# Where four prefetched weight tiles lie in an fp32 decoder trunk: two raw tiles more in spare result tiles, and a transposition moved by two k-tiles

## The chip, the cores and the metric

The kernel runs on one core of a Trainium2 chip. The metric is device time in microseconds (us) of one launch, lower is better. TensorE (PE, weight loads PEld) multiplies into PSUM banks; VectorE (DVE) and ScalarE (ACT) work elementwise; GpSimd (POOL) has a few tiny instructions; SyncE (SP) issues every load of weights, in one queue, in order. Each engine runs its own instructions in order and waits on semaphores for the others.

## The reference

Two decoder layers over 256 tokens of width 2048, all float32. Layer 0 mixes tokens by retention (8 heads, keys of 256, values of 512), layer 1 by latent attention (16 heads). After each mixer comes a SwiGLU block of width 5632, and each of the four parts is wrapped in two root-mean-square norms:

```python
h = rms_norm(x, norm_ffn_pre[i])
gate, up = jnp.split(h @ w_gu, [D_FF], axis=-1)
x = x + rms_norm((jax.nn.silu(gate) * up) @ w_down, norm_ffn_post[i])
```

The change touches retention's input products (`x @ w_in`, split into q, k, v and g) and this gate-and-up product.

## The kernel before

**Float32 by three products.** Tokens stand in two tiles of 128. Every weight tile (128 rows of k by 1024 columns, 512 KB) is loaded raw, and split into a high part (ACT, a cast) and a low part (DVE, raw minus high). A product is high x high, high x low and low x high: three matmuls of 512 columns for each token tile and each half of the columns, twelve for a k-tile.

**Groups.** The gate-and-up weights are cut into 11 groups, named `gu` 0 to 10, of 1024 columns (512 of gate, 512 of up) and 16 k-tiles. Retention has 4 query/key groups (`rqk`) and 8 value/gate groups (`rvg`). Group 0 of a kind that follows a norm runs by `group`; the others by `first_sevens`: there the first pairs of k-tiles (4 pairs in gate and up, 2 and 3 in retention) are multiplied by Strassen's scheme, with seven products instead of eight. For a pair the weights come as `s0` (a raw tile) and `s1` (a tile of tag `y4`); DVE forms the sums `ta` (L448, L452) and `t` (L449, later L463), and the parts `b`, `a`, `c`, `d`, each with hi and lo, are splits of these. In the names of the profile these are `gu_bhi`, `gu_blo` and so on. When the pairs are through, four DVE instructions combine the banks (L475, L478, L482, L485, with ACT copies L471 and L479 into `mv`). Then k-tiles 8 to 15 of gate and up follow one by one as `w8` to `w15`.

**Rings of tiles.** There are 4 raw tiles, 5 pairs of hi and lo, 6 banks of tag `mm`, of which a group takes 4, and 4 tiles of tag `y4`. A raw tile is free again when its last split or sum has been made, a hi/lo pair when its last matmul has read it.

**Spare tiles.** The result of a group's activation, transposed, is kept until the down product: 11 tiles `aT` of 128 x 1024 in gate and up (8 tiles `yT` in retention). While fewer groups are done, tiles of this ring are empty. The kernel lends them to the last k-tiles of a group for their hi and lo parts (names `xhi`, `xlo`): with j groups done, `min(2, (groups - j) // 2)` k-tiles get such a pair, so two in gate and up from group 0 to 7, one in 8 and 9, none in 10. Retention's query/key groups have two tiles of their own for this (one k-tile).

**End of a group.** For each token tile ACT makes silu of the gate bank (`fsg`), DVE multiplies with the up bank (L995, into `fa`), then TensorE transposes four blocks into a bank of tag `misc` (L962, `ftp`), and ACT copies them to `aT` (L963). The transposes are put off with `later(2 + t, ...)`: a count of k-tiles begun, so they are written down in the third and fourth k-tile of the next group. The final order of each engine is made by a scheduler from the order of writing, its priorities and free tiles; the order on each queue is shown below where it matters.

**Names in the tables:** `gu_w_raw` loads at L544, `gu_s` at L440 and L443; casts at L204, low parts at L205, all matmuls at L409.

Of the kernel before, what the change touches and what calls it, by code (L numbers as in the profile page):

```python
# [8 lines left out]
F32 = mybir.dt.float32  # L9
F32R = mybir.dt.float32r  # L10
# [5 lines left out]
P = 128  # L16
SEQ = 256
D = 2048
DT = D // P
NT = SEQ // P  # L20
EPS = 1e-6
RH, RK, RV = 8, 256, 512
# [35 lines left out]
def trunk(  # L58
# [73 lines left out]
    def later(k, fn):  # L132
        order[0] += 1
        todo.append((steps[0] + k, order[0], fn))
# [63 lines left out]
    wp = ctx.enter_context(tc.tile_pool(name="wp", bufs=1))  # L198
    RAW, WB, MV = 4, 5, 6

    def split(hi, lo, src, g=None):

        if g is None:
            nc.scalar.copy(out=hi, in_=src)  # L204
            nc.vector.tensor_sub(out=lo, in0=src, in1=hi.bitcast(F32))  # L205
        else:
            nc.scalar.activation(out=hi, in_=src, func=AF.Copy, scale=g)
            nc.vector.scalar_tensor_tensor(
                out=lo, in0=src, scalar=g, in1=hi.bitcast(F32), op0=ALU.mult, op1=ALU.subtract
            )  # L210

    def weights(load, parts, name, room=None):

        raw = wp.tile([P, 1024], F32, tag="raw", bufs=RAW, name=f"{name}_raw")
        load(raw)
        if room is None:
            hi = wp.tile([P, 1024], F32R, tag="whi", bufs=WB, name=f"{name}_hi")
            lo = wp.tile([P, 1024], F32R, tag="wlo", bufs=WB, name=f"{name}_lo")
        else:
            hi, lo = room(f"{name}_xhi"), room(f"{name}_xlo")  # L220
# [309 lines left out]
        carry_out(plan, banks, cols, {})  # L530
        return banks

    def tile_load(w, g, name, halves=0, spare=(0, None)):

        def load(kt, first_half=False):
            n = 512 if kt < halves or first_half else 1024

            def dma(raw):
                for a in range(0, 1024, 512 if kt < halves else 1024):
                    m = 512 if kt < halves else 1024
                    nc.sync.dma_start(out=raw[:, a : a + m], in_=w[g, kt, :, a : a + m])  # L544

            parts = [(a, n, None) for a in range(0, 512 if first_half else 1024, n)]
            return weights(dma, parts, f"{name}_w{kt}", spare[1] if kt >= DT - spare[0] else None)

        return load

# [186 lines left out]
    def retention():  # L737
# [40 lines left out]
        def vg_group(h, spare):  # L778
            return first_sevens(h_lhs, DT, ret_vg, h, f"rvg{h}", VG_SEVENS, lambda p: ins[p], spare)

        with tc.tile_pool(name="rt_s", bufs=1) as sp:
# [63 lines left out]
            with tc.tile_pool(name="rt_q", bufs=1) as rp:  # L845
                rope_c = rp.tile([P, NT, NF_R], F32, name="rope_c")
                rope_s = rp.tile([P, NT, NF_R], F32, name="rope_s")
                spare = 1, lambda name: rp.tile([P, 1024], F32R, tag="spare", bufs=2, name=name)
                for gq in range(4):
                    banks = qk_group(gq, spare)  # L850
                    if gq == 0:
                        rx = [rms(first[t], D, "rx", f"first_r{t}") for t in range(NT)]
                        rotary_tables()
                        for t in range(NT):
                            for dst, src in ((rope_c, cos_t), (rope_s, sin_t)):
                                nc.vector.tensor_scalar(
                                    dst[:, t, :], src[:, t, 0:NF_R], scalar1=rx[t], scalar2=None,
                                    op0=ALU.mult,
                                )
                    head_scores(gq, rotated(banks, rope_c, rope_s, rp), rp)  # L860
                banks = vg_group(0, spare)

            with tc.tile_pool(name="rt_v", bufs=1) as rp:

                yT = {}

                def spare_y(name):
                    return rp.tile([P, 1024], F32R, tag="yT", bufs=RH, name=name)

                def take_y(k0, n):  # L870
                    return yT[k0 // 4][:, k0 % 4 : k0 % 4 + n]
# [73 lines left out]
    def swiglu(i):  # L945
        with tc.tile_pool(name=f"ff{i}", bufs=1) as fp:

            groups = FF // 512
            aT = {}

            def spare_a(name):
                return fp.tile([P, 1024], F32R, tag="aT", bufs=groups, name=name)

            def take_a(k0, n):
                return aT[k0 // 4][:, k0 % 4 : k0 % 4 + n]
# [23 lines left out]

            for j in range(groups):  # L980
                name = f"gu{i}_{j}"
                spare = min(2, (groups - j) // 2), spare_a
                if j:
                    banks = first_sevens(
                        h_lhs, DT, w_gu[i], j, name, GU_SEVENS, lambda p: ins[p], spare
                    )
                else:
                    banks = group(h_lhs, DT, tile_load(w_gu[i], j, name, 0, spare), name, lead=4)
                watch[0] = None
                both = fp.tile([P, NT, 512], F32, tag="fa", bufs=1, name="fa")  # L990
                for t in range(NT):
                    sg = fp.tile([P, 512], F32, tag="fsg", bufs=2, name="fsg")
                    nc.scalar.activation(out=sg, in_=banks[t][0], func=AF.Silu, scale=rx_next[t])
                    a = both[:, t, :]
                    nc.vector.scalar_tensor_tensor(  # L995
                        out=a, in0=banks[t][1], scalar=rx_next[t], in1=sg, op0=ALU.mult, op1=ALU.mult
                    )
# [282 lines left out]


    retention()
    swiglu(0)
    mla()
    swiglu(1)


# [89 lines left out]
```

## Time and profile before

| what | value |
|---|---|
| median of 3 runs | 2427.02 us (2423.98 to 2428.43) |
| profiled execution's own time | 2426.71 us |
| span of its instructions | 2424.9 us |
| granted TensorE clock, mean over the span | 0.998 |
| busy: TensorE, DVE, ACT | 99%, 88%, 61% of the span |
| read from HBM | 459.64 MB, 190 GB/s over the span |
| gate-and-up groups 1 to 10, layer 0 and layer 1 | 426.69 us and 424.95 us |
| the seven retention value groups 1 to 7 | 313.57 us |

A line of a group or a wait names engine, line of the kernel, what is written and read, and times in us; `<-` after a bracket or a name is what ended the wait. A row of the windows view has the stretch, its length, then for PE, PEld, DVE, ACT and POOL busy us and, in brackets, the number of instructions; then the granted clock, the share of time that the 16 DMA engines were busy, and GB/s. A row of the timeline has the start, the duration, engine, line, operation, tiles and the count of equal instructions merged; in square brackets the engine's idle time before it and what ended it. Matmuls overlap: a duration of 0.39 us is that of one in the pipeline, and the pace is read from start to start.

### The profile page before, as it was taken

The numbers are of one execution on the slowest core, as the hardware profiler recorded it, in microseconds if no ns is written. First come the engines' busy times: TensorE is split into PE (matmuls) and PEld (weight loads), VectorE is DVE, ScalarE is ACT, GpSimd is POOL, SyncE is SP. The second block draws the span as 40 slices with busy tenths as digits, with TensorE's granted clock in tenths as the row PEclk, the third lists the DMA queues.
The fourth block names the chain that finished last, engine by engine and source line by source line (L and its number), as shares of the span: only waits on it lengthen the run. The fifth ranks groups of instructions, "written<-read, shape, count | busy, mean of one in ns | idle before, by whom it ended". The sixth has DMA issues, their size and how long they took to land.

```text
span 2424.9 us, 30707 instructions
## 1 busy us (share of the span) xinstructions
PE 2403.3 (99%) x10888; PEld 1975.1 (81%) x10888; DVE 2122.0 (88%) x3034; ACT 1479.1 (61%) x2082; POOL 23.9 (1%) x38
## 2 busy tenths in 40 slices
PE   9999999999999999999999999999999999999998
PEld 7888888888888787888888888888877888888887
DVE  8878989887879999899989987876899999998997
ACT  6545666665656666666666665655666666666664
POOL 0000000000000000000000000000000000000000
PEclk9999999999999999999999999999999999999999
DMA  7565565556665565656456654446656565556655
GB/s 273 171 211 185 164 206 194 165 172 203 192 213 193 195 213 184 217 172 216 168 194 214 207 185 148 130 137 198 202 182 215 180 211 202 188 183 202 206 194 164
DMA packets 129610, 463.75 MB, mean 191 GB/s; under 512 B 14640, under 2 KB 15024, under 8 KB 129456
## 3 DMA queue, kind: packets, MB, share of 16 engines
q1 hardware_dynamic: 129456, 461.80, 57.7%
q8 instruction: 85, 1.39, 0.2%
q14 instruction: 69, 0.57, 0.1%
HBM read 459.64 MB, written 2.10 MB: 190 GB/s over the span
## 4 chain that ended last, share of the span: by engine, by line
PE 80%; DVE 12%; DMA 4%; issue 2%; ACT 2%; SPq 0%; POOL 0%; DVEq 0%; ACTq 0%; POOLq 0%
PE gu_b L409 23%; PE dn_b L409 16%; PE rvg_b L409 14%; PE rto_b L409 6%; PE rqk_b L409 5%; PE mlo_b L409 3%; PE q L409 3%; PE dn_m L409 3%; DMA gu_w_raw<-w_gu 2%; DVE gu_blo L205 2%; DVE gu_alo L205 1%; PE mc_b L409 1%; DVE gu_w_lo L205 1%; DVE gu_t L449 1%; DVE gu_clo L205 1%
## 5 line engine op out<-in xcount | busy, mean ns | idle before, releaser
L409 PE MATMUL gu_b<-gu_w_hi,hT 128*128 128x512 f32 x1248 | 342.0, 390 | 0.0
L409 PEld LDWEIGHTS gu_b<-gu_w_hi,hT 128*128 128x128 f32 x1248 | 233.1, 188 | 49.0 <-DVE hT L205 0.9
L204 ACT CAST dn_w_hi<-dn_w_raw 128x1024 fp32r<-128x1024 f32 (+1 forms) x176 | 172.8, 993 | 95.2 <-DMA dn_w_raw<-w_down 44.4
L205 DVE TENSOR_TENSOR gu_w_lo<-gu_w_raw,gu_w_hi 128x1024 fp32r<-128x1024 f32 x156 | 185.5, 1218 | 48.4 <-ACT gu_w_hi L204 48.3
L204 ACT CAST gu_w_hi<-gu_w_raw 128x1024 fp32r<-128x1024 f32 x156 | 158.1, 1048 | 92.9 <-DMA gu_w_raw<-w_gu 73.2
L205 DVE TENSOR_TENSOR dn_w_lo<-dn_w_raw,dn_w_hi 128x1024 fp32r<-128x1024 f32 (+1 forms) x176 | 196.1, 1146 | 9.2 <-ACT dn_w_hi L204 8.9
L409 PE MATMUL gu_b<-gu_w_lo,hT 128*128 128x512 f32 x624 | 193.3, 390 | 0.0
L409 PE MATMUL dn_b<-dn_w_hi,dn_ah 128*128 128x512 f32 x536 | 169.3, 390 | 0.0
L409 PE MATMUL dn_b<-dn_w_lo,dn_ah 128*128 128x512 f32 x536 | 169.0, 389 | 0.0
L409 PE MATMUL dn_b<-dn_w_hi,dn_al 128*128 128x512 f32 x536 | 168.9, 389 | 0.0
L409 PE MATMUL rvg_b<-rvg_w_hi,hT 128*128 128x512 f32 x552 | 149.8, 390 | 0.0
L409 PEld LDWEIGHTS gu_b<-gu_w_lo,hT 128*128 128x128 f32 x624 | 116.6, 188 | 25.3 <-DVE gu_w_lo L205 1.3
L409 PEld LDWEIGHTS rvg_b<-rvg_w_hi,hT 128*128 128x128 f32 x552 | 103.4, 188 | 21.4
L409 PEld LDWEIGHTS dn_b<-dn_w_hi,dn_al 128*128 128x128 f32 x536 | 100.6, 188 | 21.0
L409 PEld LDWEIGHTS dn_b<-dn_w_lo,dn_ah 128*128 128x128 f32 x536 | 100.6, 188 | 20.9
L409 PEld LDWEIGHTS dn_b<-dn_w_hi,dn_ah 128*128 128x128 f32 x536 | 100.3, 188 | 20.4
L409 PE MATMUL rqk_b<-rqk_w_hi,hT 128*128 128x512 f32 x384 | 106.0, 392 | 2.2 <-ACT rqk_w_hi L204 1.5
L204 ACT CAST gu_ahi<-gu_ta 128x1024 fp32r<-128x1024 f32 x80 | 84.3, 1054 | 35.1 <-DVE gu_ta L452 17.1
L205 DVE TENSOR_TENSOR rvg_w_lo<-rvg_w_raw,rvg_w_hi 128x1024 fp32r<-128x1024 f32 x69 | 82.3, 1222 | 25.5 <-ACT rvg_w_hi L204 25.1
L204 ACT CAST gu_bhi<-gu_t 128x512 fp32r<-128x512 f32 x80 | 49.7, 621 | 85.9 <-DVE gu_t L449 85.8
L204 ACT CAST rvg_w_hi<-rvg_w_raw 128x1024 fp32r<-128x1024 f32 x69 | 71.1, 1051 | 46.0 <-DMA rvg_w_raw<-ret_vg 34.7
L205 DVE TENSOR_TENSOR gu_alo<-gu_ta,gu_ahi 128x1024 fp32r<-128x1024 f32 x80 | 97.7, 1221 | 0.0
(487 smaller groups left out, 6109.5 us busy)
## 6 DMA issues: line engine op xcount, KB each, us to landing
gu_w_raw<-w_gu SPq DMA_DIRECT2D x192, 512.0 KB, 4.3
dn_w_raw<-w_down SPq DMA_DIRECT2D x176, 512.0 KB, 4.4
gu_s<-w_gu SPq DMA_DIRECT2D x160, 512.0 KB, 4.4
rvg_w_raw<-ret_vg SPq DMA_DIRECT2D x80, 512.0 KB, 4.4
rto_w_raw<-ret_out SPq DMA_DIRECT2D x64, 512.0 KB, 4.4
rqk_w_raw<-ret_qk SPq DMA_DIRECT2D x51, 512.0 KB, 4.5
rvg_s<-ret_vg SPq DMA_DIRECT2D x48, 512.0 KB, 4.3
mlo_w_raw<-mla_out SPq DMA_DIRECT2D x32, 512.0 KB, 3.6
```

Of the source, the lines that this page charges most:

```text
L204: nc.scalar.copy(out=hi, in_=src)
L205: nc.vector.tensor_sub(out=lo, in0=src, in1=hi.bitcast(F32))
L409: nc.tensor.matmul(out, e[2](), e[3](), start=bank not in begun, stop=ends[bank, added.get(bank, 0)] == n, skip_group_check=bank in added,)
L449: nc.vector.tensor_add(out=t2[p], in0=ta[:, 0:512], in1=b11)
```

## The change

A function `share(slots, room)` replaces the two-tile rule. With `slots` empty result tiles it gives `both` k-tiles a hi/lo pair (two from 6 slots on, one from 3 on, else none), and up to two of the remaining tiles hold **raw** weights (names `xraw`): of k-tiles 12 and 13, or of 13 alone. Gate and up thus have 2 pairs and 2 raws in groups 0 to 5, 1 pair and 2 raws in 6 and 7, 1 and 1 in 8, 0 and 2 in 9, 0 and 1 in 10. Retention's value groups 1 and 2 have 2 and 2, 3 and 4 have 1 and 2, 5 has 1 and 1, 6 has 0 and 2, 7 has 0 and 1. The query/key groups and value group 0 get a third tile: 1 pair and 1 raw. And the transposes of the gate-and-up activations are put off by `later(4 + t, ...)`.

```diff
+    def share(slots, room):
+        both = 2 if slots >= 6 else 1 if slots >= 3 else 0
+        return min(2, slots - 2 * both), both, room
...
-    def weights(load, parts, name, room=None):
-        raw = wp.tile([P, 1024], F32, tag="raw", bufs=RAW, name=f"{name}_raw")
+    def weights(load, parts, name, raw_room=None, room=None):
+        if raw_room is None:
+            raw = wp.tile([P, 1024], F32, tag="raw", bufs=RAW, name=f"{name}_raw")
+        else:
+            raw = raw_room(F32, f"{name}_xraw")
...
-            return weights(dma, parts, f"{name}_w{kt}", spare[1] if kt >= DT - spare[0] else None)
+            raws, both, room = spare
+            return weights(
+                dma, parts, f"{name}_w{kt}", room if DT - 2 - raws <= kt < DT - 2 else None,
+                room if kt >= DT - both else None,
+            )
...
-                spare = 1, lambda name: rp.tile([P, 1024], F32R, tag="spare", bufs=2, name=name)
+                spare = share(3, lambda kind, name: rp.tile([P, 1024], kind, tag="spare", bufs=3, name=name))
...
-                        banks = vg_group(h, (min(2, (RH - h) // 2), spare_y))
+                        banks = vg_group(h, share(RH - h, spare_y))
...
-                spare = min(2, (groups - j) // 2), spare_a
+                spare = share(groups - j, spare_a)
...
-                    later(2 + t, lambda j=j, t=t, a=a: transposes(j, t, a))
+                    later(4 + t, lambda j=j, t=t, a=a: transposes(j, t, a))
```

No instruction is added or removed, and none changes its size. The scheduler makes a new order from it. Lines move too: L440, L443 and L544 become L449, L452 and L554; L205, L449, L452, L463 and L995 become L210, L458, L461, L472 and L1009; L409 and L962 become L418 and L976.

**SyncE's queue from group 5 to group 6 of layer 0.** `gu_5_w_raw` are k-tiles 8 to 11 and then 12 to 15; of the `gu_6_s` loads the first four are `s1`, the last four `s0` of the next group. Before:

```order
L544 DMA gu_5_w_raw<-w_gu 128x1024 x4
L443 DMA gu_6_s_8833<-w_gu 128x1024
L443 DMA gu_6_s_8874<-w_gu 128x1024
L443 DMA gu_6_s_8905<-w_gu 128x1024
L443 DMA gu_6_s_8936<-w_gu 128x1024
L544 DMA gu_5_w_raw<-w_gu 128x1024 x4
L440 DMA gu_6_s_8831<-w_gu 128x1024
```

Of the change:

```order
L554 DMA gu_5_w_raw<-w_gu 128x1024 x4
L554 DMA gu_5_w_xraw<-w_gu 128x1024 x2
L452 DMA gu_6_s_8833<-w_gu 128x1024
L452 DMA gu_6_s_8861<-w_gu 128x1024
L452 DMA gu_6_s_8905<-w_gu 128x1024
L452 DMA gu_6_s_8936<-w_gu 128x1024
L554 DMA gu_5_w_raw<-w_gu 128x1024 x2
L449 DMA gu_6_s_8831<-w_gu 128x1024
```

The loads of k-tiles 12 and 13 moved ahead of the four `s1` loads; 14 and 15 stayed behind them.

**DVE where the activation of group 5 is made, among the sums and low parts of group 6.** `fa` is the activation, `s_8934` and `s_8936` belong to the fourth pair. Before:

```order
L205 TENSOR_TENSOR gu_6_blo<-gu_6_s_8903,gu_6_bhi 128x512
L452 TENSOR_TENSOR gu_6_ta<-gu_6_s_8903,gu_6_s_8905 128x512
L205 TENSOR_TENSOR gu_6_blo<-gu_6_t_8908,gu_6_bhi 128x512
L448 TENSOR_TENSOR gu_6_ta<-gu_6_s_8934 128x512
L995 SCALAR_TENSOR_TENSOR fa<-gu_5_b_8460,rto_x_r,fsg 128x512
L449 TENSOR_TENSOR gu_6_t_8939<-gu_6_ta,gu_6_s_8936 128x512
L995 SCALAR_TENSOR_TENSOR fa<-gu_5_b_8462,rto_x_r,fsg 128x512
L452 TENSOR_TENSOR gu_6_ta<-gu_6_s_8934,gu_6_s_8936 128x512
L463 TENSOR_TENSOR gu_6_t_8836<-gu_6_t_8836,gu_6_s_8833 128x512
L205 TENSOR_TENSOR gu_6_alo<-gu_6_ta,gu_6_ahi 128x1024
```

Of the change:

```order
L210 TENSOR_TENSOR gu_6_blo<-gu_6_t_8908,gu_6_bhi 128x512
L457 TENSOR_TENSOR gu_6_ta<-gu_6_s_8934 128x512
L461 TENSOR_TENSOR gu_6_ta<-gu_6_s_8934,gu_6_s_8936 128x512
L458 TENSOR_TENSOR gu_6_t_8939<-gu_6_ta,gu_6_s_8936 128x512
L472 TENSOR_TENSOR gu_6_t_8836<-gu_6_t_8836,gu_6_s_8833 128x512
L472 TENSOR_TENSOR gu_6_t_8864<-gu_6_t_8864,gu_6_s_8861 128x512
L1009 SCALAR_TENSOR_TENSOR fa<-gu_5_b_8460,rto_x_r,fsg 128x512
L472 TENSOR_TENSOR gu_6_t_8908<-gu_6_t_8908,gu_6_s_8905 128x512
L1009 SCALAR_TENSOR_TENSOR fa<-gu_5_b_8462,rto_x_r,fsg 128x512
L210 TENSOR_TENSOR gu_6_alo<-gu_6_ta,gu_6_ahi 128x1024
```

The two activations moved behind the sums of the fourth pair and behind three of the four L463 (now L472).

**TensorE in the first pairs of group 6.** `ftp` are the transposes of group 5's activation. Before:

```order
L409 MATMUL gu_6_b_8829<-gu_6_alo,sh_6615 128x512
L409 MATMUL gu_6_b_8829<-gu_6_ahi,sl_6616 128x512
L962 MATMUL ftp_8860<-cst,fa 128x128 x4
L962 MATMUL ftp_8868<-cst,fa 128x128 x4
L409 MATMUL gu_6_b_8827<-gu_6_bhi,hT 128x512
```

Of the change:

```order
L418 MATMUL gu_6_b_8830<-gu_6_alo,sh_6615 128x512
L418 MATMUL gu_6_b_8830<-gu_6_ahi,sl_6616 128x512
L976 MATMUL ftp_8891<-cst,fa 128x128 x4
L976 MATMUL ftp_8899<-cst,fa 128x128 x4
L418 MATMUL gu_6_b_8827<-gu_6_bhi,hT 128x512
```

The transposes moved from behind the first pair's nine matmuls to behind the second pair's twelve; the bank `b_8830`, which the second pair is the first to write, now comes ahead of them. Later in groups 1 to 4 of both layers the `chi,sh` matmuls now stand ahead of the first `dhi,hT` one, as they did in groups 5 to 10; in group 10 it is the other way round.

More of the change, by code (lines that the diff above doesn't have):

```diff
@@ L219, in weights @@
         else:
-            hi, lo = room(f"{name}_xhi"), room(f"{name}_xlo")
+            hi, lo = room(F32R, f"{name}_xhi"), room(F32R, f"{name}_xlo")
         for a, n, g in parts:
@@ L531, in first_sevens, with tile_load @@
         return banks
-    def tile_load(w, g, name, halves=0, spare=(0, None)):
+    def tile_load(w, g, name, halves=0, spare=(0, 0, None)):
         def load(kt, first_half=False):
@@ L865, in retention, with spare_y @@
                 yT = {}
-                def spare_y(name):
-                    return rp.tile([P, 1024], F32R, tag="yT", bufs=RH, name=name)
+                def spare_y(kind, name):
+                    return rp.tile([P, 1024], kind, tag="yT", bufs=RH, name=name)
                 def take_y(k0, n):
@@ L949, in swiglu, with spare_a @@
             aT = {}
-            def spare_a(name):
-                return fp.tile([P, 1024], F32R, tag="aT", bufs=groups, name=name)
+            def spare_a(kind, name):
+                return fp.tile([P, 1024], kind, tag="aT", bufs=groups, name=name)
             def take_a(k0, n):
```

## The prediction

> **What bounds the kernel now.** I read the page first, then the list of waits of TensorE's loads, then the windows of single groups, then the timeline of one group's end. The page says that TensorE is busy 99% of the span. So I ask first which stages have TensorE time to give back at all.
>
> ```profile
> PE 2403.3 (99%) x10888; PEld 1975.1 (81%) x10888; DVE 2122.0 (88%) x3034; ACT 1479.1 (61%) x2082; POOL 23.9 (1%) x38
> PEld gu_b L409 <- ACT gu_mv L479: 5.8, 8, 0.9
> PEld ftp L962 <- DVE fa L995: 5.3, 13, 0.8
> PEld gu_b L409 <- DVE gu_b L482: 5.3, 12, 0.7
> PEld gu_b L409 <- DVE gu_clo L205: 2.7, 7, 0.5
> PEld gu_b L409 <- DVE gu_dlo L205: 1.7, 3, 0.7
> ACT gu_w_hi L204 <- DMA gu_w_raw<-w_gu: 73.2, 45, 3.4
> ```
>
> The five PEld lines (total us, times, longest) are the longest waits of TensorE inside the gate-and-up groups: all for VectorE (DVE), or for a ScalarE (ACT) copy behind it. The last line is of ACT, and comes back below. They hold the 0.04 to 0.23 us that lie before any load, so their sum is too high. The loss itself I take from lengths of groups. The first three rows below are groups 1, 6 and 7 of the first layer, from one first matmul to the next; the two "sum" rows add groups 1 to 10 of the first and of the second layer; the fourth is the seven value-and-gate groups of retention.
>
> ```profile
> 780.84:823.83 42.99, 42.40 (x190) 34.38 (x188) 40.76 (x54) 27.54 (x37) 0.00 (x0) 1.00 0.56 197
> 995.19:1037.04 41.85, 41.85 (x189) 34.51 (x188) 38.08 (x49) 26.34 (x34) 0.00 (x0) 1.00 0.62 201
> 1037.04:1080.13 43.09, 42.46 (x189) 34.40 (x188) 39.99 (x52) 27.06 (x36) 0.00 (x0) 1.00 0.61 196
> sum 313.57, PE 313.57 PEld 257.35 DVE 275.20 ACT 197.04 POOL 7.70; mean PE 44.80 PEld 36.76 DVE 39.31 ACT 28.15 POOL 1.10
> sum 426.69, PE 422.95 PEld 344.52 DVE 396.93 ACT 268.97 POOL 0.00; mean PE 42.30 PEld 34.45 DVE 39.69 ACT 26.90 POOL 0.00
> sum 424.95, PE 423.25 PEld 344.37 DVE 395.96 ACT 269.88 POOL 0.00; mean PE 42.32 PEld 34.44 DVE 39.60 ACT 26.99 POOL 0.00
> 1223.61 11.56 PE dn_b L409 x51
> ```
>
> The last row, of the chain, gives the pace of matmuls that wait for nothing: 11.56 / 51 = 0.227 us. A group has 180 of them and eight small transposes: 40.8 us plus about 1. Group 6, where TensorE was never idle, took 41.85; I take that as the floor. The twenty groups took 426.69 + 424.95 = 851.6, and 20 x 41.85 = 837.0: **14.6 us, 0.6% of the span, is all that better feeding of these groups can return.** In retention's groups TensorE is busy for 313.57 of 313.57 us: nothing is there to win. DVE needs 39.6 us a group on average, under the floor: it is late in places, not too slow in sum.
>
> Where is it late? DVE's timeline at the end of group 6 and the start of group 7:
>
> ```profile
> 1013.20 4.62 DVE L205 TENSOR_TENSOR gu_w_lo<-gu_w_raw,gu_w_hi 128x1024 fp32r<-128x1024 f32 x4
> 1019.03 1.23 DVE L205 TENSOR_TENSOR gu_w_lo<-gu_w_raw,gu_w_hi 128x1024 fp32r<-128x1024 f32 x1 [1.20 <-ACT gu_w_hi L204]
> 1021.27 1.23 DVE L205 TENSOR_TENSOR gu_w_lo<-gu_w_raw,gu_w_hi 128x1024 fp32r<-128x1024 f32 x1 [1.01 <-ACT gu_w_hi L204]
> 1025.24 1.23 DVE L205 TENSOR_TENSOR gu_w_xlo<-gu_w_raw,gu_w_xhi 128x1024 fp32r<-128x1024 f32 x1 [1.46 <-ACT gu_w_xhi L204]
> 1026.38 0.69 DVE L448 TENSOR_TENSOR gu_ta<-gu_s 128x512 f32<-128x512 f32 x1
> 1038.46 0.75 DVE L995 SCALAR_TENSOR_TENSOR fa<-gu_b,rto_x_r,fsg 128x512 f32<-128x512 f32 x1
> 1039.72 0.74 DVE L995 SCALAR_TENSOR_TENSOR fa<-gu_b,rto_x_r,fsg 128x512 f32<-128x512 f32 x1
> 1051.59 0.69 DVE L482 TENSOR_TENSOR gu_b<-gu_b,gu_mv 128x512 f32<-128x512 f32 x1
> 1017.95 1.05 ACT L204 CAST gu_w_hi<-gu_w_raw 128x1024 fp32r<-128x1024 f32 x1 [2.66 <-DMA gu_w_raw<-w_gu]
> 1024.16 1.05 ACT L204 CAST gu_w_xhi<-gu_w_raw 128x1024 fp32r<-128x1024 f32 x1 [1.63 <-DMA gu_w_raw<-w_gu]
> 1014.45 3.73 SPq L544 DMA_DIRECT2D gu_w_raw<-w_gu  x4
> ```
>
> Read from the bottom. SyncE issues the loads of k-tiles 12 to 15 at 1014.45, right when the low part of tile 8 is done (1013.20 + 1.22): there are four raw tiles, and tile 12 must have tile 8's. The loads land too late for ACT (waits of 2.66 and 1.63), so DVE idles 1.20 + 1.01 + 1.46 = 3.7 us, starts the next group's sums (L448) only at 1026.38, and is then busy without a break. TensorE feels it at two places of group 7:
>
> ```profile
> 1037.04 0.39 PE L409 MATMUL gu_b<-gu_bhi,hT 128*128 128x512 f32 x1
> 1038.85 0.39 PE L409 MATMUL gu_b<-gu_ahi,sl 128*128 128x512 f32 x1
> 1039.26 0.65 PE L962 MATMUL ftp<-cst,fa 128*128 128x128 f32 x4
> 1040.52 0.66 PE L962 MATMUL ftp<-cst,fa 128*128 128x128 f32 x4 [0.60 <-DVE fa L995]
> 1040.93 0.47 PE L409 MATMUL gu_b<-gu_bhi,hT 128*128 128x512 f32 x1
> 1049.90 0.39 PE L409 MATMUL gu_b<-gu_chi,hT 128*128 128x512 f32 x1
> 1052.33 0.50 PE L409 MATMUL gu_b<-gu_chi,sh 128*128 128x512 f32 x1
> ```
>
> From 1038.85 to 1040.93 are 2.08 us for one matmul (0.227) and eight transposes (about 0.11 each, 0.87): 1.0 us is lost to L995. From 1049.90 to 1052.33 are 2.43 for nine matmuls (2.04): 0.4 is lost to L482, which ends at 1052.28.
>
> **The change, part by part.** Counts are the same; instructions and loads only move.
>
> *Two raw tiles in spare result tiles (gate and up).* Tiles 12 and 13 no longer wait for the ring: their loads go out behind that of tile 11 and are there long before ACT wants them at 1015.3 (1017.95 less its wait of 2.66), when it is through with tile 11's cast. Tiles 14 and 15 get the ring slots of 8 and 9, the next group's first two loads those of 10 and 11. DVE's eight low parts then run on: four to 1017.8, four more at 1.13 each (the first row's pace) to 1022.4. The next group starts at about 1022.5 instead of 1026.38: a lead of 3.9 us (an estimate from these rows). It holds only as far as the five hi/lo tiles let it: the third pair's first tile needs the slot of k-tile 13. TensorE takes 12 x 0.227 = 2.72 for a k-tile; eight of them end at 1037.04, so tile 13 is done at 1037.04 - 2 x 2.72 = 1031.6. The third pair's parts can thus start at about 1032 and the lead is not cut there.
>
> Two more loads now stand ahead of four others in SyncE's queue. These windows show the engines when they move:
>
> ```profile
> 995.19:1001.50 6.31, 6.31 (x33) 5.33 (x32) 6.31 (x11) 4.40 (x7) 0.00 (x0) 1.00 0.26 83
> 1001.50:1005.00 3.50, 3.50 (x17) 2.89 (x16) 3.46 (x5) 2.89 (x4) 0.00 (x0) 1.00 0.49 150
> 1014.45:1024.13 9.68, 9.68 (x45) 8.00 (x44) 7.05 (x6) 3.99 (x4) 0.00 (x0) 1.00 0.80 275
> ```
>
> Two transfers leave a stretch with a DMA share of 0.80 for one of 0.26 to 0.49. The four loads behind them are wanted at 1023 or later and went out from 1005 on: cost nothing, even if each came 2 x 1.9 us later (1 MB at 275 GB/s is 3.8). The Trainium skill, DMA: Bandwidth & Descriptors, "Issuing engines are not separate DMA queues", says that all transfers end on the same 16 engines, so that starting more at once wins no bandwidth. By that rule, if the engines were full, the late loads would stay late and the sum would be that of the no-lead rival below. No row here has a share of 1.00, so the trace speaks against its applying.
>
> *Transposes two k-tiles later.* On TensorE they stand 12 matmuls later, 2.72 us. On DVE four more instructions stand ahead of each L995 (L452 and three L463 ahead of the second). From L995 to L995, with one between them, are 1.26 us, 0.6 a step: 4 x 0.6 = 2.4 us. So the move itself is nearly even; with the lead L995 is ready as soon as its banks are, about 1038.8 for the second half, and the transposes ask at 1037.04 + 21 x 0.227 = 1041.8. The 19th matmul of the group takes a bank that the first L995 frees; it asks at 1041.1 and gets it by 1037.7. The cover is 3 us of other matmuls; without it the 1.0 us would be back. What is late next is the L482 chain: TensorE asks at 1037.04 + 57 x 0.227 + 0.9 = 1050.9; following DVE on from the third pair (third and fourth parts are released by TensorE's own progress) I get its end between 1050.6 and 1051. I leave 0.1 us per group for it.
>
> *Fewer spare hi/lo tiles.* Groups 6 and 7 give up one of two, group 9 its only one, and groups 7, 8 and 10 may start their splits one k-tile (2.72) later. In 7 and 8 the lead pays for it. Group 10 I count worse: in the new order a `dhi` matmul that waits for the L479 copy behind L478 stands first, where `chi,sh` stood. Bounds: 0 to 2.72 us each; I take 0.8, near the 5.8 / 8 = 0.7 of the L479 line above, the eight groups that have this pattern now.
>
> *Retention.* One more spare in the query/key groups, raws in the value groups: TensorE does not wait there, so nothing is gained; the first query/key group after the tables takes 48.46 us, 1.4 more than the next two, and may move by that either way.
>
> ```profile
> 56.95:105.41 48.46, 47.88 (x219) 38.80 (x218) 40.82 (x56) 23.82 (x29) 0.00 (x0) 1.00 0.58 191
> 105.41:152.49 47.08, 47.00 (x220) 39.00 (x218) 38.42 (x53) 23.39 (x28) 0.00 (x0) 1.00 0.56 187
> 1165.13:1207.53 42.40, 42.24 (x190) 34.49 (x189) 40.44 (x68) 27.82 (x36) 0.00 (x0) 1.00 0.47 156
> 1759.57:1802.68 43.11, 42.72 (x190) 34.36 (x188) 40.61 (x53) 28.17 (x38) 0.00 (x0) 1.00 0.56 198
> 2142.28:2184.52 42.24, 42.23 (x190) 34.48 (x188) 39.20 (x67) 27.58 (x36) 0.00 (x0) 1.00 0.46 150
> ```
>
> **The sum.** Over the floor are: both groups 1, 42.99 + 43.11 - 83.70 = 2.4; both groups 10, 42.40 + 42.24 - 83.70 = 0.9; so groups 2 to 9 hold 14.6 - 3.3 = 11.3. There 16 x 0.1 stays: -9.7. Groups 1 lose their transposes' wait and part of the `dlo` wait: -0.9. Groups 10: +1.6. Net -9.0 on the profiled execution's 2426.71: 2417.7. The median of the runs is 0.3 higher: **2418 us**.
>
> **The rivals.** *No lead.* The raws come early but DVE stays where it is, because the next loads are late or the hi/lo slots come from TensorE later than I reckon; then the move alone decides, 2.72 against 2.4: 0 to 2 us gained, 2426. For it: ACT and DVE wait for each other all along; against it: the idle 3.7 us end on loads alone. *The lead reaches everything.* All twenty groups at the floor: 2427 - 14.6 = 2412. Against it: the L482 chain has no margin in my working. *Hi/lo tiles decide, and it is slower.* Groups 7, 8 and 10 of both layers and retention's groups 4, 5 and 7 follow a group that gave up a pair. If their splits hang on TensorE's release, each pays up to a k-tile: 9 x 2.72 = 24.5. At 60% that is 14.7, less the 7 us that groups 2 to 6 and 9 still win: 2435. It decides from about 0.8 us a group on. Against it: DVE has 41.85 - 39.6 = 2.2 us of slack in a group, and both groups 10 followed a group with one pair before and lasted 42.40 and 42.24, under the mean of 851.6 / 20 = 42.6.
>
> **The numbers.** Forecast 0.60, no lead 0.19, all at the floor 0.12, slower 0.09. The range of 8 in 10 goes from the floor to the no-lead case: 2411 to 2426; the forecast's own, with 0 to 0.4 us left per group and 0 to 2.7 for groups 10, is 2413 to 2423. What a measurement can tell from no change is 0.2%, 4.9 us: faster 0.72, same 0.20, slower 0.08 (a slow case may also end within 0.2%).
>
> **What would show it.** Right: the waits of `ftp` for `fa` vanish; DVE's first L448 of a group starts about 4 us before it does now, measured from the group's first matmul; waits of ACT for `gu_w_raw` fall from 73 us to a third; groups 2 to 9 last 41.8 to 42.1. Wrong: DVE idle for ACT's casts moves to the next group's parts, `gu_b` waits for `blo` or `alo`, or groups 7, 8 and 10 become the longest.

## The result and the profile after

The change takes 2410.70 us (median; 2408.57 to 2413.81) where the kernel before took 2427.72 (2423.98 to 2429.53) beside it: a ratio of 0.9933, 95% interval 0.9916 to 0.995. The forecast was 2418 with a range of 2411 to 2426. The direction is as forecast; the time lies 0.3 us below the range's low end, and the gain is about twice what was summed. The profiled execution took 2408.57 us with a span of 2406.8, so 18.1 us less than the span before; the terms below are made against these two.

First the page: the busy time of each engine, two waits of TensorE's loads inside gate and up, and two lines of ACT (total us, times, longest).

```profile
PE 2390.7 (99%) x10888; PEld 1976.6 (82%) x10888; DVE 2120.9 (88%) x3034; ACT 1472.3 (61%) x2082; POOL 27.0 (1%) x38
PEld gu_b L418 <- DVE gu_b L491: 1.1, 2, 0.7
PEld gu_b L418 <- ACT gu_mv L488: 0.8, 2, 0.4
ACT gu_bhi L209 <- PE gu_b L418: 64.0, 56, 1.7
ACT gu_w_hi L209 <- DMA gu_w_raw<-w_gu: 14.2, 8, 3.8
```

`ftp` for `fa` (5.3 us, 13 times) is gone, the L482 wait (now L491) fell from 12 times to 2, that for the ACT copy from 8 to 2. ACT waited 73.2 us for raw weights ahead of these casts and now waits 14.2; with the casts into spare tiles (`gu_w_xhi`: 16.1 before, 18.7 now) it is 89.3 and 32.9, about a third. Instead ACT waits for TensorE to give back the hi/lo tiles of `gu_bhi` (64.0 us, 13.4 before): the engines that make parts are now ahead of the one that uses them.

The windows of groups 1, 7 and 10 of the first layer, the sums of groups 1 to 10 of both layers, and of retention's value groups 1 to 7; last a piece of the chain of waits (the 180 matmuls from the transposes of one group to those of the next, released by nothing but themselves):

```profile
780.05:822.38 42.33, 42.08 (x190) 34.46 (x189) 42.33 (x57) 27.19 (x37) 0.00 (x0) 1.00 0.63 211
1031.13:1072.88 41.75, 41.75 (x189) 34.59 (x188) 39.71 (x52) 26.50 (x35) 0.00 (x0) 1.00 0.59 202
1156.39:1198.37 41.98, 41.98 (x190) 34.54 (x188) 40.79 (x68) 28.22 (x37) 0.00 (x0) 1.00 0.48 163
sum 418.32, PE 418.07 PEld 345.75 DVE 396.58 ACT 266.93 POOL 0.00; mean PE 41.81 PEld 34.58 DVE 39.66 ACT 26.69 POOL 0.00
sum 418.17, PE 418.17 PEld 345.76 DVE 395.95 ACT 268.01 POOL 0.00; mean PE 41.82 PEld 34.58 DVE 39.59 ACT 26.80 POOL 0.00
sum 312.95, PE 312.95 PEld 257.35 DVE 272.80 ACT 195.12 POOL 7.68; mean PE 44.71 PEld 36.76 DVE 38.97 ACT 27.87 POOL 1.10
2088.46 40.89 PE gu_b L418 x180
```

Group 7 took 43.09 and takes 41.75. All sixteen groups from 2 to 9 now last 41.73 to 41.79. That is TensorE's own work: 40.89 for 180 matmuls and 8 x 0.11 for the transposes make 41.77. DVE's work did not shrink (396.58 against 396.93).

How the end of group 6 looks now, to set beside the two timelines of the prediction. One row of the kernel before that was not shown yet comes first: the loads of `s0`, the first four of the next group.

```profile
1020.29 6.53 SPq L440 DMA_DIRECT2D gu_s<-w_gu  x4
```

And the change: SyncE, DVE, TensorE.

```profile
1008.51 1.46 SPq L554 DMA_DIRECT2D gu_w_raw<-w_gu  x2
1010.79 8.15 SPq L449 DMA_DIRECT2D gu_s<-w_gu  x4
1015.62 1.23 DVE L210 TENSOR_TENSOR gu_w_xlo<-gu_w_raw,gu_w_xhi 128x1024 fp32r<-128x1024 f32 x1 [1.02 <-ACT gu_w_xhi L209]
1016.76 0.68 DVE L457 TENSOR_TENSOR gu_ta<-gu_s 128x512 f32<-128x512 f32 x1
1017.36 1.22 DVE L210 TENSOR_TENSOR gu_w_lo<-gu_w_raw,gu_w_hi 128x1024 fp32r<-128x1024 f32 x1
1032.99 0.75 DVE L1009 SCALAR_TENSOR_TENSOR fa<-gu_b,rto_x_r,fsg 128x512 f32<-128x512 f32 x1
1035.89 1.03 PE L976 MATMUL ftp<-cst,fa 128*128 128x128 f32 x8
```

Group 7 begins at 1031.13 here and began at 1037.04 before. Call **lead** the time from the start of DVE's first sum for a group (L448, now L457) to that group's first matmul: 1037.04 - 1026.38 = 10.66 before, 1031.13 - 1016.76 = 14.37 now, 3.7 us more. The late raw loads go out 22.6 us ahead of the group in both (1037.04 - 1014.45, 1031.13 - 1008.51), but they are two now, not four, and `s0` follows them 20.3 us ahead instead of 16.75. The traces show why. Before, the first `s0` load needs the raw tile of k-tile 12 and goes out when its low part ends (1019.03 + 1.23 = 1020.26), which is late itself. Now it gets the tile of k-tile 10, the third of four low parts that DVE begins at 1007.26 and makes every 1.14 us (end at about 1010.76). The load landed 5.1 us after its issue before and 5.0 now, about 1 us ahead of DVE's first sum both times. DVE makes its first sum while the last low part of the old group is still to come (1017.36). The second activation ends at 1033.74, 2.1 us before the transposes want it.

### The profile page after: what moved, and what is told of

It is laid out like the page before. It is cut to its first block, busy times and chain, and to the rows that moved or that the text cites. A ratio compares the mean times of both kernels' runs of the same rounds, so it can differ in the third digit from the quotient of the medians.

```text
span 2406.8 us, 30784 instructions
## 1 busy us (share of the span) xinstructions
PE 2390.7 (99%) x10888; PEld 1976.6 (82%) x10888; DVE 2120.9 (88%) x3034; ACT 1472.3 (61%) x2082; POOL 27.0 (1%) x38
## 4 chain that ended last, share of the span: by engine, by line
PE 94%; DVE 3%; DMA 1%; issue 1%; ACT 1%; SPq 0%; DVEq 0%; POOLq 0%; POOL 0%; ACTq 0%
PE gu_b L418 37%; PE dn_b L418 16%; PE rvg_b L418 14%; PE rto_b L418 6%; PE rqk_b L418 4%; PE mlo_b L418 4%; PE q L418 3%; PE dn_m L418 3%; PE mc_b L418 1%; PE ftp L976 1%; PE ry L896 1%; PE rto_m L418 1%; PE asc L1228 0%; PE asc L1225 0%; DVE rqk_w_lo L210 0%
## 5 line engine op out<-in xcount | busy, mean ns | idle before, releaser
L418 PE MATMUL gu_b<-gu_w_hi,hT 128*128 128x512 f32 x1296 | 353.5, 390 | 0.0
L418 PEld LDWEIGHTS gu_b<-gu_w_hi,hT 128*128 128x128 f32 x1296 | 242.1, 188 | 50.8 <-DVE hT L210 0.9
L210 DVE TENSOR_TENSOR dn_w_lo<-dn_w_raw,dn_w_hi 128x1024 fp32r<-128x1024 f32 (+1 forms) x176 | 196.7, 1149 | 14.9 <-ACT dn_w_hi L209 14.6
L418 PE MATMUL gu_b<-gu_w_lo,hT 128*128 128x512 f32 x648 | 200.2, 390 | 0.0
L418 PE MATMUL dn_b<-dn_w_hi,dn_ah 128*128 128x512 f32 x536 | 169.1, 389 | 0.0
L418 PE MATMUL dn_b<-dn_w_hi,dn_al 128*128 128x512 f32 x536 | 168.9, 389 | 0.0
L418 PE MATMUL dn_b<-dn_w_lo,dn_ah 128*128 128x512 f32 x536 | 168.9, 389 | 0.0
L418 PE MATMUL rvg_b<-rvg_w_hi,hT 128*128 128x512 f32 x576 | 156.5, 390 | 0.0
L210 DVE TENSOR_TENSOR gu_w_lo<-gu_w_raw,gu_w_hi 128x1024 fp32r<-128x1024 f32 x122 | 143.5, 1223 | 8.1 <-ACT gu_w_hi L209 8.1
L418 PEld LDWEIGHTS gu_b<-gu_w_lo,hT 128*128 128x128 f32 x648 | 121.1, 188 | 26.2 <-DVE gu_w_lo L210 1.3
L209 ACT CAST gu_w_hi<-gu_w_raw 128x1024 fp32r<-128x1024 f32 x122 | 122.5, 1050 | 31.1 <-DMA gu_w_raw<-w_gu 14.2
L418 PEld LDWEIGHTS rvg_b<-rvg_w_hi,hT 128*128 128x128 f32 x576 | 107.8, 188 | 22.3
L418 PEld LDWEIGHTS dn_b<-dn_w_hi,dn_ah 128*128 128x128 f32 x536 | 100.6, 188 | 20.9
L418 PEld LDWEIGHTS dn_b<-dn_w_lo,dn_ah 128*128 128x128 f32 x536 | 100.6, 188 | 20.9
L418 PEld LDWEIGHTS dn_b<-dn_w_hi,dn_al 128*128 128x128 f32 x536 | 100.6, 188 | 20.8
L210 DVE TENSOR_TENSOR gu_clo<-gu_s,gu_chi 128x1024 fp32r<-128x1024 f32 x80 | 97.6, 1222 | 14.5 <-ACT gu_chi L209 13.1
L418 PE MATMUL rqk_b<-rqk_w_hi,hT 128*128 128x512 f32 x384 | 106.0, 392 | 1.9 <-ACT rqk_w_hi L209 1.5
L210 DVE TENSOR_TENSOR gu_alo<-gu_ta,gu_ahi 128x1024 fp32r<-128x1024 f32 x80 | 97.9, 1223 | 7.2 <-ACT gu_ahi L209 7.0
L209 ACT CAST gu_bhi<-gu_s 128x512 fp32r<-128x512 f32 x80 | 49.7, 622 | 77.7 <-PE gu_b L418 64.0
L209 ACT CAST gu_chi<-gu_s 128x1024 fp32r<-128x1024 f32 x80 | 83.8, 1051 | 13.5 <-PE gu_b L418 13.4
```

Of the source, the lines that this page charges most:

```text
L418: nc.tensor.matmul(out, e[2](), e[3](), start=bank not in begun, stop=ends[bank, added.get(bank, 0)] == n, skip_group_check=bank in added,)
```

## The experiments

Lead is read as above; a group's length is from its first matmul to the next group's.

**The transposes back in their old place.**

```diff
-                    later(4 + t, lambda j=j, t=t, a=a: transposes(j, t, a))
+                    later(2 + t, lambda j=j, t=t, a=a: transposes(j, t, a))
```

> The raw tiles without the move: the change with the transposes put back to two and three k-tiles (2 + t). Lead theory: DVE's idle of 3.7 us a group on late loads stays gone and the groups keep most of the gain of 15.2 us; only the transposes come 2.72 us too early and meet the second activation, 0 to 0.6 us in each of 20 groups. About 2414 us (2410 to 2419), groups 2 to 9 between 41.75 and 42.3. Rival, the move does it: with the old place of the transposes the waits of ftp for fa come back whole (13 of them, 5.3 us) and the rest with them: 2420 or more.

2412.69 us (2410.95 to 2414.61), ratio 0.9938 (0.9926 to 0.9951). The wait of `ftp`, the sums of both layers and group 3:

```profile
PEld ftp L976 <- DVE fa L1009: 2.2, 6, 0.8
sum 420.23, PE 419.19 PEld 345.49 DVE 397.68 ACT 269.09 POOL 0.00; mean PE 41.92 PEld 34.55 DVE 39.77 ACT 26.91 POOL 0.00
sum 418.27, PE 418.27 PEld 345.58 DVE 395.38 ACT 268.76 POOL 0.00; mean PE 41.83 PEld 34.56 DVE 39.54 ACT 26.88 POOL 0.00
865.00:907.78 42.78, 42.18 (x190) 34.49 (x188) 40.94 (x54) 26.85 (x35) 0.00 (x0) 1.00 0.62 212
```

The raw tiles alone bring 13.1 of the change's 15.15 us in these groups. Where the old place costs, it costs at the second activation: in group 3 it ends 3.39 us after the group's start, and the second four transposes ask for it at 2.5.

**The move alone**, in the kernel before.

```diff
-                    later(2 + t, lambda j=j, t=t, a=a: transposes(j, t, a))
+                    later(4 + t, lambda j=j, t=t, a=a: transposes(j, t, a))
```

> The move without the raw tiles: the kernel before with the transposes put off by 4 + t. Lead theory: DVE still idles on the late loads of k-tiles 12 to 15 and the activations move back on DVE nearly as far (2.4 us by estimate) as the transposes on TensorE (2.72): 2425 us (2421 to 2429), DVE's waits for casts and ACT's waits of some 70 us for gu_w_raw stay. Rival, the move does it: the ftp waits for fa (5.3 us) vanish and little else was needed: 2420 or less.

2426.41 us (2422.95 to 2427.63), ratio 0.9991 (0.9982 to 1.0): no difference. Its waits and sums:

```profile
PEld gu_b L409 <- DVE gu_clo L205: 7.2, 14, 1.2
PEld gu_b L409 <- DVE gu_b L482: 6.3, 11, 0.7
sum 427.09, PE 422.98 PEld 343.97 DVE 396.45 ACT 267.02 POOL 0.00; mean PE 42.30 PEld 34.40 DVE 39.65 ACT 26.70 POOL 0.00
sum 424.99, PE 421.54 PEld 344.58 DVE 395.18 ACT 267.84 POOL 0.00; mean PE 42.15 PEld 34.46 DVE 39.52 ACT 26.78 POOL 0.00
```

The 5.3 us of `ftp` for `fa` are gone, and the groups last as long as before (426.69 and 424.95): the same lateness of DVE is now met a few matmuls later, at `gu_clo` (2.7 us before, 7.2 now) and at L482. A wait shows where lateness is met, not where it arises. Also, the second activation ends on average 2.65 us after the group's start, against 2.53 before: the scheduler left it where it was in DVE's order, and the 2.4 us that were expected did not come.

**Raw tiles for k-tiles 14 and 15 instead of 12 and 13.**

```diff
-                dma, parts, f"{name}_w{kt}", room if DT - 2 - raws <= kt < DT - 2 else None,
+                dma, parts, f"{name}_w{kt}", room if kt >= DT - raws else None,
```

> As many raw tiles in spare result tiles, but given to k-tiles 14 and 15 instead of 12 and 13, so that 12 and 13 still wait for the raw ring's tiles of k-tiles 8 and 9. Lead theory, its cause being the ring: casts of 12 and 13 come late as before, DVE idles 1.2 us and more before them, and the lead shrinks from 3.9 us to less than half: 2417 to 2426 us, ACT's waits for raw loads above 40 us in sum. Rival, any two raw tiles more do it (the next group's first two loads get their places earlier): within 3 us of the change, 2408 to 2414.

2414.30 us (2411.41 to 2416.03), ratio 0.9943 (0.993 to 0.9955). ACT's wait for raw weights, the loads at the end of group 6, DVE's first sum for group 7 (which begins at 1031.19), and the two sums:

```profile
ACT gu_w_hi L209 <- DMA gu_w_raw<-w_gu: 76.7, 45, 4.0
1008.56 1.47 SPq L554 DMA_DIRECT2D gu_w_raw<-w_gu  x2
1010.83 6.21 SPq L449 DMA_DIRECT2D gu_s<-w_gu  x4
1017.56 0.69 DVE L457 TENSOR_TENSOR gu_ta<-gu_s 128x512 f32<-128x512 f32 x1 [0.87 <-DMA gu_s<-w_gu]
sum 418.85, PE 418.17 PEld 345.78 DVE 396.87 ACT 265.77 POOL 0.00; mean PE 41.82 PEld 34.58 DVE 39.69 ACT 26.58 POOL 0.00
sum 419.30, PE 418.22 PEld 345.78 DVE 396.88 ACT 267.29 POOL 0.00; mean PE 41.82 PEld 34.58 DVE 39.69 ACT 26.73 POOL 0.00
```

The rival holds here, not my theory, though the median is 0.3 us over the rival's range too (2.4 us over the change by the two ratios). Tiles 12 and 13 are as late as ever (loads 22.6 us ahead of the group, 76.7 us of waiting), yet all groups 2 to 9 last 41.69 to 41.77. What both places have in common is SyncE's queue: two late loads, then `s0` 20.4 us ahead of the group. DVE fills its gaps with the next group's sums; the one shown waited 0.87 us for `s0` itself. So it is the number of raw places, through the time of `s0`, that gives the lead. What it lacks to the change lies, in the profiles, in the groups 1 (42.98 and 43.31, against 42.33 and 42.16) and 0 (48.13 and 48.28 against 47.45 and 47.51), and 0.6 us in the latent input product. The groups 1 are uncertain by themselves: in a second profile of the change they took 42.67 and 43.03.

**Retention alone**: gate and up with the old counts of pairs, no raw tiles and the old place of the transposes.

```diff
-                spare = share(groups - j, spare_a)
+                spare = 0, min(2, (groups - j) // 2), spare_a
```

> The share of spare tiles in retention alone; gate and up and the transposes as before. By the prediction retention has nothing to gain (TensorE busy for 313.57 of 313.57 us): 2426 us (2424 to 2429), the gate-and-up groups as before. Rival: some of the 18 us came from retention or from what follows it, then 2424 or less.

2424.68 us (2422.36 to 2427.13), ratio 0.999 (0.9981 to 0.9998): some 2.4 us by the ratio. That is inside the expected range by 0.7 us, but the interval leaves out 1, so the rival has a point. Gate and up has none of it (425.35 + 426.11 = 851.46, before 851.64), and the value groups have little:

```profile
sum 313.06, PE 313.06 PEld 257.36 DVE 274.12 ACT 195.11 POOL 7.70; mean PE 44.72 PEld 36.77 DVE 39.16 ACT 27.87 POOL 1.10
```

That is 0.5 us. In its profile 2.35 us more are missing in the latent input product of layer 1 (54.29 against 56.64), which the edit does not touch; see the last section.

**One raw tile instead of two.**

```diff
-        return min(2, slots - 2 * both), both, room
+        return min(1, slots - 2 * both), both, room
```

> The change with one raw tile (k-tile 13) in the spare tiles instead of two. Lead here is how long before a group's first matmul DVE starts that group's first sum; in the traces so far a gate-and-up group lasts 41.75 us where the lead is 12 us or more and about 41.75 + (12.0 - lead) where it is less (before: leads 10.7 to 11.9; the change: 12.5 to 15). Threshold theory: one raw tile gives leads of 12.3 to 13, as group 9 of the change has behind a group with one, so groups 2 to 9 stay at 41.7 to 41.9 and the time is 2410 to 2414 us. Proportional rival, the gain goes with the number of tiles: half of it, 2417 to 2421 us.

2412.08 us (2410.77 to 2413.37), ratio 0.9931 (0.9919 to 0.9944). The leads of groups 2 to 9 are 11.7 to 12.9 us, their lengths 41.69 to 42.02. One tile brings nearly all, as the threshold theory has it. The groups 1 lose (43.57 and 43.18).

**The old number of hi/lo pairs**, raw tiles only from what is left.

```diff
-        both = 2 if slots >= 6 else 1 if slots >= 3 else 0
+        both = min(2, slots // 2)
```

> The change with as many hi/lo pairs as before (half of the spare tiles, at most two), raw tiles only where one is left over: groups 6, 8 and 10 then have one, groups 7 and 9 none. Lead theory: the group behind one without a raw tile starts with a lead of about 11.2 us as before, so groups 8 and 10 last 42.2 to 42.6 where the change has 41.76 and 41.98; the others stay; together 2 us: 2411 to 2415 us. Rival, hi/lo pairs decide the late groups: groups 7 to 10 get no worse than in the change, or better: 2408 to 2411.

2412.38 us (2410.70 to 2414.81), ratio 0.9934 (0.9921 to 0.9948). Groups 8 and 10 of the first layer, then group 8 of the second:

```profile
1074.91:1116.98 42.07, 42.01 (x190) 34.49 (x188) 39.96 (x52) 26.65 (x35) 0.00 (x0) 1.00 0.58 200
1158.71:1200.95 42.24, 42.06 (x189) 34.51 (x188) 41.07 (x69) 27.46 (x36) 0.00 (x0) 1.00 0.47 162
2043.61:2086.30 42.69, 42.30 (x190) 34.42 (x188) 40.45 (x54) 26.53 (x36) 0.00 (x0) 1.00 0.60 197
```

Of groups 2 to 10 only those behind one without a raw tile got longer (group 10 of the second layer, 42.19, is the fourth). The leads of the three shown are 11.5, 11.3 and 10.9 us. So the rival of the hi/lo pairs fell here.

**No hi/lo pair in spare tiles at all.**

```diff
-        both = 2 if slots >= 6 else 1 if slots >= 3 else 0
+        both = 0
```

> The change with no hi/lo pair in spare tiles at all: only raw tiles for k-tiles 12 and 13, in every group of gate and up and of retention. Raw theory: the hi/lo ring of five is enough (group 10 of the change starts with a lead of 14.9 us behind a group without a pair), so gate and up stays at 41.75 a group: 2409 to 2414 us, retention within 1 us. Rival, hi/lo pairs decide: the first parts of the next group wait one or two k-tiles of 2.72 us longer for a slot, leads fall to 9 to 12 us and groups 2 to 7 lose 1 us and more each: 2420 us or more.

2413.87 us (2413.76 to 2416.23), ratio 0.9941 (0.9928 to 0.9955). Sums of both layers and of retention's value groups:

```profile
sum 420.34, PE 419.88 PEld 345.36 DVE 394.97 ACT 265.73 POOL 0.00; mean PE 41.99 PEld 34.54 DVE 39.50 ACT 26.57 POOL 0.00
sum 420.08, PE 419.83 PEld 345.36 DVE 394.58 ACT 266.44 POOL 0.00; mean PE 41.98 PEld 34.54 DVE 39.46 ACT 26.64 POOL 0.00
sum 311.29, PE 311.29 PEld 257.78 DVE 275.11 ACT 193.12 POOL 7.70; mean PE 44.47 PEld 36.83 DVE 39.30 ACT 27.59 POOL 1.10
```

The rival that hi/lo tiles decide has fallen: leads stay at 13.8 to 15.8 us behind the first group. But the groups do not stay at 41.75 either, as the raw theory expected: each lasts 41.97 to 42.21. In the trace each now has the order in which `dhi,hT` comes first, as group 10 of the change has, with one wait for the L488 copy in each of the 20 groups (8.7 us in sum): 0.23 us over the floor. Retention's value groups 1 to 7 without pairs are up to 0.4 shorter each (1.7 in sum), but two query/key groups (47.8 against 47.07) and value group 0 (48.17 against 46.42) lose that again and more.

**Up to four raw tiles.**

```diff
-        return min(2, slots - 2 * both), both, room
+        return min(4, slots - 2 * both), both, room
```

> The change with up to four raw tiles (k-tiles 10 to 13) where the spare tiles allow it (groups 0 to 2 of gate and up; groups 3 to 8 get those left over). Threshold theory: groups 2 to 9 stand on the floor of 41.75 us (180 matmuls of 0.227 and eight transposes of 0.11), more lead buys nothing; only group 1 (0.6 and 0.4 us above it) can win: 2409 to 2412 us, no difference from the change. Rival, more loads ahead still help: below 2408.

2408.68 us (2408.28 to 2409.86), ratio 0.9918 (0.9905 to 0.9932). Gate and up is 0.6 us under the change (417.91 + 418.02), all of it in the groups 1; the floor holds. In the first layer group 0 takes 1.1 us more in exchange (48.56 against 47.45). The median is 0.3 us under what was expected; its interval and that of the change overlap, so no difference is shown.

**Three more sums a group on DVE**, in the change and in the kernel before, written ahead of the first sum of a group (L457, there L448). In the traces the scheduler put one or two of the three ahead of it and the rest within 1.8 us behind it; they start 0.60 us apart, so they add 1.8 us a group:

```diff
+            if p == 0 and name.startswith("gu"):
+                for _ in range(3):
+                    nc.vector.tensor_add(out=ta[:, 512:1024], in0=b00, in1=b01)
             nc.vector.tensor_add(out=ta[:, 0:512], in0=b00, in1=b01)
```

> The change with work added to DVE: three more sums of 128x512 (the form of L457, 0.68 us busy, about 0.6 from start to start) ahead of the first sum of gate-and-up groups 1 to 10, 1.9 us a group, results overwritten. The leads of 13.7 to 14.8 us shrink to about 12 to 13, and DVE has 2 to 4 us idle a group. Reserve theory: 12.0 us of lead is enough, so most groups stay within 0.3 us of 41.75 and the whole costs 0 to 8 us: 2411 to 2419 us. Rival, DVE's time sets the end directly: 20 x 1.9 = 38 us more, about 2449 us.

> The same three sums a group in the kernel before. Its leads of 10.7 to 11.9 us are already under 12.0, so there is no reserve: each group gets up to 1.9 us longer, 20 x 1.9 = 38 us at most, 20 at least if DVE's idle on late loads takes a part: 2447 to 2466 us. Rival, DVE's idle of 3 to 4 us a group absorbs the 1.9: within 6 us of before, under 2434 us.

The change with them: 2418.57 us (2414.74 to 2420.30), 8 more than the change. The kernel before with them: 2470.09 (2469.24 to 2471.39), 43.6 more than before, and more than the 38 that I had called the most. The sums of both layers, the change with the three sums first:

```profile
sum 423.09, PE 420.87 PEld 344.98 DVE 413.17 ACT 267.42 POOL 0.00; mean PE 42.09 PEld 34.50 DVE 41.32 ACT 26.74 POOL 0.00
sum 421.29, PE 419.88 PEld 345.23 DVE 410.93 ACT 266.93 POOL 0.00; mean PE 41.99 PEld 34.52 DVE 41.09 ACT 26.69 POOL 0.00
```

And the kernel before with them:

```profile
sum 447.66, PE 436.88 PEld 340.46 DVE 412.73 ACT 264.05 POOL 0.00; mean PE 43.69 PEld 34.05 DVE 41.27 ACT 26.40 POOL 0.00
sum 446.97, PE 435.86 PEld 340.77 DVE 412.75 ACT 264.12 POOL 0.00; mean PE 43.59 PEld 34.08 DVE 41.27 ACT 26.41 POOL 0.00
```

DVE is equally busy in both (41.1 to 41.3 us a group). In the change the sixteen groups 2 to 9 pay 2.9 us for 16 x 1.8 = 29 us of added work, their leads being 11.4 to 14.0; most of the other 5 us of the change lies in the groups 1 (45.30 and 43.54). In the kernel before the sixteen pay 36 (358.59 + 358.54 against 341.30 + 339.60), with leads of 7.0 to 9.8. That is the reserve that the change built up, measured; before there was none. Why the kernel before pays more than the work that was added stays open.

**A further version and the change once more**: four raw tiles in gate and up, and in retention's value groups raw tiles only.

```diff
-                        banks = vg_group(h, share(RH - h, spare_y))
+                        banks = vg_group(h, (min(4, RH - h), 0, spare_y))
```

> Up to four raw tiles in gate and up (as in the run with four), and in retention's value groups 1 to 7 up to four raw tiles and no hi/lo pair; without pairs these groups lasted 44.47 us where the change has 44.47 to 44.85. By the sum of groups: 1.9 us less in retention than the change, 0 to 0.5 less in gate and up: 2408 to 2410 us if the time of other stages stays. Rival, a group's 0.3 us is chance of the order: 2410 to 2412, no difference.

> The change itself once more, as the measure for the other runs of this call: 2409 to 2413 us; groups 2 to 9 of gate and up at 41.75. Whether the latent input product (54.75 us in the change's profile, 56.64 in that of before, with a granted clock of 0.51 for 3.35 us of it) keeps its length: by the theory that it is chance, 54 to 57 us.

On the same chip: 2408.09 us (2405.79 to 2409.16) against 2410.62 (2409.98 to 2412.29) for the change, ratios to before 0.9921 (0.9908 to 0.9933) and 0.9933 (0.9921 to 0.9946). The ranges do not meet, so it is some 2.5 us faster than the change, though the intervals overlap. The value groups give 1.4 us (311.58 against 313.00), the groups 1 to 10 of gate and up 1.9, and the two groups 0 give 2.6 back (48.73 and 48.57 against 47.32 and 47.36). These parts explain 0.7 of the 2.5 us; where the rest lies is not shown. Two raw tiles in group 0 and four behind it were not tried. The change's latent input product took 55.23 us this time.

## Why the prediction was half the size

**The lead is the cause** in groups 2 to 9. The table has 160 groups (2 to 9 of both layers) in ten profiles: before, the change twice, and the runs with the move alone, raw tiles last, retention alone, one raw, old pairs, four raws, and the further version. Length by lead:

| lead, us | groups | mean length | range |
|---|---|---|---|
| under 10.0 | 3 | 43.45 | 43.03 to 43.83 |
| 10.0 to 10.5 | 7 | 42.98 | 42.48 to 43.33 |
| 10.5 to 11.0 | 7 | 42.75 | 42.42 to 43.09 |
| 11.0 to 11.5 | 24 | 42.45 | 42.13 to 42.73 |
| 11.5 to 12.0 | 12 | 41.93 | 41.72 to 42.19 |
| 12.0 to 13.0 | 27 | 41.74 | 41.69 to 41.77 |
| 13.0 and more | 80 | 41.75 | 41.69 to 41.79 |

From 12 us on nothing more is won. Below that, each microsecond of lead that is missing costs some 0.7 to 0.9 us (42.75 at about 10.75: 1.0 for 1.25). Left out are the profiles with other work or another order (added sums, no pairs, old place of the transposes). In the last of these two groups with leads of 13.1 and 14.3 lasted 42.78 and 42.08: the lead suffices only with the transposes moved. The groups 1 do not follow the table either: 41.87 at a lead of 11.3 with four raw tiles, 42.33 at 12.5 in the change, 43.43 at 11.9 with the old pairs. What else sets them is open.

What the lead hangs on is `s0`, and the traces show it. In 128 of these groups, those of the eight profiles with at most two raw tiles, DVE's first sum starts 0.02 to 1.86 us after the first `s0` load of the group has landed (half of them within 0.8). In the kernel before that load landed 11.6 us ahead of group 7, so the lead there could not have been 14.4. With four raw tiles `s0` lands up to 19.3 us ahead, and no lead is over 15.9: something else limits it there, which no run isolates.

By the prediction's own terms, in the two profiles:

| term | forecast | measured |
|---|---|---|
| gate and up, groups 2 to 9 | -9.7 | -12.9 |
| groups 1 | -0.9 | -1.6 |
| groups 10 | +1.6 | -0.7 |
| retention's value groups 0 to 7 | 0 | -1.0 |
| latent input product | not named | -1.9 |
| sum | -9.0 | -18.1 |

- *A lead of 3.9 us*: 3.7 in group 7. Right in size.
- *"DVE idles 1.20 + 1.01 + 1.46"*, because 12 and 13 wait for the ring's tiles: half the reason. The raw ring was the cause, but the run with tiles 14 and 15 shows that the loads' lateness may stay; what must come earlier is `s0`. The prediction gives "the next group's first two loads" the ring tiles of 10 and 11, but works the lead out from DVE's low parts alone and leaves `s0` without a term; its 3.6 us of earlier issue were what counted. (The four loads called "wanted at 1023 or later" and of no cost are those of `s1`, and of them that is right.)
- *The floor of 41.85*: mis-sized. It is 41.75; group 6 had a lead of 11.92 and was itself 0.1 late. Sixteen groups make 1.6 us. Another 1.6 is the 0.1 left for L482 in each group: with 2.4 us of lead in reserve nothing was left.
- *Groups 10, +0.8 each*: wrong in sign. The order with `dhi` first costs 0.23 (41.98 against 41.75, and as much in every group of the run without pairs), not the 0.7 of the L479 waits; with the lead the same wait is 0.4 on average (8.7 us in 20 groups without pairs, 0.8 in 2 in the change), so part of the 0.7 was DVE's lateness seen at another place. The lead pays more than the order costs.
- *The transposes*: "the move itself is nearly even" is right in effect (no difference alone) and wrong in its working. DVE's activations do not move 2.4 us with it (2.65 against 2.53). It is the raw tiles that move them in DVE's order; with the lead they still end as early as before or earlier on average (2.15 in the run with the old place, 2.11 in the change), and the transposes' 2.72 us are needed as cover in the few groups where one is late. Worth: 1 to 2 us in the groups (838.50 without the move, 836.49 and 837.59 with it).
- *Retention, nothing to win*: 0.6 us in value groups 1 to 7 (312.95, and 313.00 in the second profile, against 313.57, and 313.52 with the move alone), although TensorE shows as busy throughout. The other 0.4 of the row is value group 0 (46.42 against 46.83) and is not the change's: with the move alone, where retention is as before, it lasts 46.40. Busy for 313.57 of 313.57 us is no proof of a floor: matmuls last 0.39 us and start 0.227 apart, so a delay of up to 0.16 need leave no idle time.
- *The rivals*: "the lead reaches everything" (2412, given 0.12) came nearest. It holds for groups 2 to 9 and not for 1 and 10, and the floor itself was lower. "No lead" and "hi/lo tiles decide" fell by the sums and by the run without pairs.

## What to carry to other kernels

Look for how early the first instruction of a stage's feeder runs ahead of the stage, and plot the stage's length against it over all its repetitions: a knee tells the floor, the price of each microsecond and the reserve, while a list of waits tells only where lateness is met. When a ring of buffers is short by a few, ask which load is next in the in-order queue behind those that wait: freeing any two places may serve as well as the two that are seen waiting. To show a reserve, add a known amount of work to both versions and compare what each pays.

## What was not expected of the hardware

The latent input product has a pause of TensorE of some 2 us for `hT`. Windows of it: the kernel before (pause, then the matmuls behind it), and the run with raw tiles last:

```profile
1455.50:1458.15 2.65, 0.66 (x4) 0.23 (x2) 1.58 (x4) 2.05 (x6) 0.00 (x0) 1.00 0.83 284
1458.15:1461.50 3.35, 3.35 (x8) 2.67 (x9) 3.08 (x4) 1.67 (x8) 0.00 (x0) 0.51 0.48 166
```

```profile
1446.30:1449.32 3.02, 0.66 (x5) 0.23 (x3) 2.25 (x5) 2.06 (x7) 0.00 (x0) 1.00 0.92 309
1449.32:1452.50 3.18, 3.18 (x14) 2.65 (x15) 3.18 (x5) 2.74 (x9) 0.00 (x0) 1.00 0.54 175
```

In the first the granted clock fell to 0.51 for 3.35 us, with 8 matmuls where the other has 14: 3.35 x 0.49 = 1.6 of the 1.9 us of this stage. In the second it did not, though its pause was longer (2.5 us from one matmul to the next beyond the usual, against 2.2). Over all fourteen profiles the pauses are 2.2 to 2.8 us where it fell and 1.1 to 2.8 where it did not, so the length of the pause alone does not decide. The drop is in four profiles of fourteen (before, the move alone, before with three sums, no pairs), and these are all those in which retention has no raw tile beside a pair; engines have the same order there in the kernel before and in the run with retention alone. The Trainium skill, TensorE: Matmul & The Clock Gate, "What's actually happening", speaks of a free-running window of 3.4 us on whose activity the clock depends. The length of the drop agrees with that, the pauses are shorter than such a window. Why the drop goes with retention's tiles is open, and one profile each is little to tell it from chance. That retention alone was 2.4 us faster over 11 launches, with 0.5 of it in the value groups, speaks for more than chance.
